# Three scattered edits around the end of an attention loop: stores on another queue, a norm eleven steps later, a diagonal built in two halves

## The chip, the core and the metric

The program runs on one core of one Trainium2 chip. The metric is device time in microseconds (us). A core has five engines that each work through their own instructions in program order: TensorE (PE, matmuls; PEld is its weight load), VectorE (DVE), ScalarE (ACT), GpSimd (POOL) and SyncE (SP). SP computes nothing here: it issues DMA transfers, one behind the other, and an issue that has to wait holds up all that stand behind it. ACT and POOL can issue DMAs too, between their own computations. Operands lie in SBUF, matmul results in PSUM, which has eight banks of 128x512 float32.

## The reference

One encoder layer for 2048 tokens of width 1024, in float32: a mixer with 8 stick-breaking heads and 8 chunked softmax heads, and a squared-ReLU MLP, each behind an RMS norm with shift, scale and gate from a conditioning vector.

```python
h = rmsnorm(x, g_norm1) * (1.0 + sc1) + sh1
proj = h @ w_in                                # q, k, v of both kinds of head
# stick-breaking head: s < t strictly
log_beta, log_1m = log_sigmoid(z), where(strict, log_sigmoid(-z), 0)
w = where(strict, exp(log_beta + (reverse_cumsum(log_1m) - log_1m)), 0);  o_sb = w @ v
# softmax head: own chunk of 64 and the 8 before it, relative bias
o_ca = softmax(q k / 8 + bias) @ v
x = x + gt1 * (concat(o_sb, o_ca) @ w_o)
h = rmsnorm(x, g_norm2) * (1.0 + sc2) + sh2
x = x + gt2 * (square(relu(h @ w1)) @ w2)
```

## The kernel before, in words

Float32 products are made from high and low parts: ACT casts the high part (`wth`, `os`), DVE or POOL subtracts it for the low part (`wtl`), and three matmuls go over the parts. The kernel has three stages: projections (0 to about 425 us), attention (to about 1277 us) and, behind the rest of the output projection, the MLP (to 2524 us).

**Groups and units.** The 2048 tokens are four groups of 512, g = 0 to 3. The attention loop takes the groups 2 and 3 together, then 1, then 0. For a group it runs 8 stick-breaking heads and then 8 softmax heads. A unit of work is one head of one group (for stick-breaking heads, against one block of 512 keys); it has four steps. A step issues score matmuls (`z`, or `ct` and `cz` for softmax), the soft part, and, eight steps later, four or eight transposes (`wt`) and products with the values (`acc`). In a stick-breaking step the soft part is a sigmoid on ACT, a scan on DVE (`p`) and a difference on POOL (`b`). In a softmax step it is a score with bias on DVE (`s`, with `cols` for row values), an exponential on ACT (`e`) and a multiply on POOL (`e<-e,cols`). The last group, g = 0, has one unit for each head, and its softmax heads are the end of the loop.

**Filler.** Each step also issues some matmuls of other work, so that PE has something to do while soft parts are under way. In the last group this is the output projection of group 1: eight tiles `po`, 24 matmuls each, with a weight tile `ow` each; a finished tile is added to the residual by DVE (`xr<-po`, line 229) and stored. What is left of it when the steps are through is issued behind them, and then the projection of group 0 (`pso`) from tiles `opm` that are read back from memory, then the MLP (`ps`).

**A head's result.** `finish` (line 746) puts two heads together in a tile `o` on POOL; `keep` (line 770) splits it into `os` (ACT casts, POOL subtracts) and stores it to `scr_m`, 512 KB, from SP's queue (line 775); only the very last unit uses ACT's queue. `opm` reads these stores.

**The second norm.** For groups 2 and 3 the squares of the projected rows are summed while the projection runs (`finish_row`, line 1160). When the eighth row is in, a chain of jobs follows: `second` makes four column sums on PE (`pvm`); `powers` forms mean and inverse root on four columns (`nvm` on DVE, five tiny POOL operations on `nym` and `ntm`); `spread` multiplies the identity by them on DVE (`ndgm`, 128x512, both inputs in SBUF); `third` spreads the result over the partitions with four matmuls (`prm`); and DVE copies it to SBUF (`r`). `later.add(n, job)` runs a job n steps from now. Groups 0 and 1 have their norm in the MLP, by other code.

**Banks.** Four PSUM banks (tag `z`) serve `z`, `ct`, `cz` and `wt`. Two (tag `ps`) serve `po`, `pvm` and `prm`; a tile that wants one waits until the tile before in it has been read. Two more hold `acc`.

**Order.** ACT, DVE, POOL and PE keep the order in which the code issues (their instructions all show the helper's line 42). SP's order is set by a scheduler that places each DMA.

Of the kernel before, what the change touches and what calls it, by code (L numbers as in the profile page):

```python
# [9 lines left out]
F32 = mybir.dt.float32  # L10
# [3 lines left out]
ALU = mybir.AluOpType  # L14
# [4 lines left out]
P = 128  # L19
# [6 lines left out]
TB = 512  # L26
# [53 lines left out]
def encoder_kernel(ctx, tc, xs, c, g1, g2, w_in, w_first, w_rest, gqk, bias, w_o, w1, w2, w_ada, b_ada, out):  # L80
    nc = tc.nc
    act, dve, pool, sp = nc.scalar, nc.vector, nc.gpsimd, nc.sync
# [34 lines left out]
    ident = cpool.tile([P, P], F32, name="ident")  # L117
# [21 lines left out]
    later = Later()  # L139

    def split(hi, lo, src, lo_eng=None):
        act.copy(hi, src)
        (lo_eng or dve).tensor_tensor(lo, src, hi.bitcast(F32), op=ALU.subtract)
# [22 lines left out]
    def norm_columns(pp, acc, tg):  # L166
        pv = pp.tile([P, TB], F32, tag="ps", name=f"pv{tg}")
        for i in range(4):
            pe.matmul(pv[:, i : i + 1], acc[:, i * P : (i + 1) * P], ones[:, 0:1], start=True, stop=True)
        return pv  # L170

    def norm_powers(pl, pv, tg):
        v = pl.tile([P, 4], F32, tag="nv", name=f"nv{tg}")
        dve.tensor_scalar(v, pv[:, 0:4], 1.0 / D, EPS, op0=ALU.mult, op1=ALU.add)
        y = pl.tile([P, 4], F32, tag="ny", name=f"ny{tg}")
        t = pl.tile([P, 4], F32, tag="nt", name=f"nt{tg}")
        rsqrt(y, v, t)
        return y

    def norm_diagonal(pl, y, tg, home=None):  # L180
        if home is None:
            dg = pl.tile([P, 4, P], F32, tag="ndg", name=f"ndg{tg}", bufs=1)
        else:
            dg = home.rearrange("p (a b) -> p a b", b=P)
        dve.tensor_tensor(
            dg, ident.unsqueeze(1).to_broadcast([P, 4, P]), y.unsqueeze(2).to_broadcast([P, 4, P]), op=ALU.mult
        )
        return dg
# [40 lines left out]
    def residual(g, n, ps, xr):  # L229
        dve.scalar_tensor_tensor(xr, ps, mod[:, 2 * KT + n : 2 * KT + n + 1], xr, op0=ALU.mult, op1=ALU.add)  # L230
        stores.append(lambda: sp.dma_start(scr_x[g, n], xr))
# [12 lines left out]
    if True:  # L244
# [252 lines left out]
        act, dve, pool = (Ordered(tc, e) for e in (act, dve, pool))  # L497
# [70 lines left out]
        dg = np_.tile([P, 4, P], F32, tag="ndg", name="ndga3", bufs=1)  # L568
# [61 lines left out]
        sp = osp  # L630
# [78 lines left out]
    if True:  # L709
# [7 lines left out]
        sp = nc.sync  # L717
# [28 lines left out]
        def finish(u):  # L746
            r = (u.h % 2) * HD
            q = HD - r
            if u.h % 2 == 0:
                pend["o", u.g] = op.tile([P, TB], F32, tag="o", name=f"o{u.nm}")  # L750
            o = pend["o", u.g]
            tmp = op.tile([P, TB], F32, tag="otmp", name=f"otmp{u.nm}")
            rows = slice(r, r + HD)
            act.copy(tmp[rows, :], u.acc[q : q + HD, :])

            def rest():
                act.copy(o[rows, :], u.acc[rows, :])
                soon.append(add)

            def add():  # L760
                pool.tensor_tensor(o[rows, :], o[rows, :], tmp[rows, :], op=ALU.add)
                if u.h % 2:
                    wait({3: 6, 0: 2}.get(u.g, 4), lambda: keep(u, o))

            soon.append(rest)
# [4 lines left out]
        def keep(u, o):  # L770

            os = fp.tile([P, 2, TB], F32R, tag="st", name=f"os{u.nm}")
            split(os[:, 0, :], os[:, 1, :], o, pool)
            q = act if u is units[-1] else sp
            q.dma_start(scr_m[u.g, u.ca * 4 + u.h // 2], os.bitcast(F32))
            if u.ca and u.h == NH - 1 and u.g > 0:
                filler.append(Filler(outproj, u.g))
# [382 lines left out]
        def finish_row(g, n, ps, xr):  # L1160

            residual(g, n, ps, xr)
            if g < 2 and drain:
                return
            stores.pop()()
            if g < 2:
                return

            def square():
                sq = rows[g] if n == 0 else op.tile([P, TB], F32, tag="otmp", name=f"sq{g}_{n}")  # L1170
                act.activation(sq, xr, AF.Square)
                if n:
                    soon.append(lambda: add(sq))

            def add(sq):
                pool.tensor_tensor(rows[g], rows[g], sq, op=ALU.add)
                if n == KT - 1:
                    later.add(3, second)

            def second():  # L1180
                pv = norm_columns(dense, rows[g], f"m{g}")

                def powers():
                    y = norm_powers(op, pv, f"m{g}")
                    later.add(2, lambda: spread(y))

                later.add(1, powers)

            def spread(y):
                dg = norm_diagonal(op, y, f"m{g}", op.tile([P, TB], F32, tag="otmp", name=f"ndgm{g}"))  # L1190
                later.add(2, lambda: third(dg))

            def third(dg):
                pr = dense.tile([P, TB], F32, tag="ps", name=f"prm{g}")
                for i in range(4):
                    pe.matmul(pr[:, i * P : (i + 1) * P], ones, dg[:, i, :], start=True, stop=True)
                later.add(1, lambda: dve.tensor_copy(rows[g], pr))

            if n == 0:
                rows[g] = rp.tile([P, TB], F32, tag="r", name=f"r{g}")  # L1200
            soon.append(square)
# [5 lines left out]
        units = []  # L1207
# [103 lines left out]
        op = ph.enter_context(tc.tile_pool(name="op", bufs=2))  # L1311
# [14 lines left out]
        for i in range(len(steps) + LAG):  # L1326
# [33 lines left out]
            if i + 1 < len(steps):  # L1360
                u, st = steps[i + 1]
# [8 lines left out]
    sp = osp  # L1370
# [21 lines left out]
    if True:  # L1392
# [375 lines left out]
        def plain(mb, i):  # L1768

            f = len(steps)  # L1770
            steps.extend(Second(mb, i, j) for j in range(NP))
            if i == 6:
                for n, step in enumerate((4, 5, 6, 12)):
                    update(mb, n, f + step, temp, False)
            return f
# [139 lines left out]
        def outer(i, plan):  # L1915

            f = len(steps)
            steps.extend(Outer(i, q, k) for q in range(7) for k in range(HP))
            for g in range(HP // 2):
                for pr, (begin, gap) in plan["load"].items():  # L1920
                    at(begin + gap * g, lambda pr=pr, g=g: half(i, pr, g))
                for pr, (begin, gap) in plan["sum"].items():
                    at(begin + gap * g, lambda pr=pr, g=g: half_sum(i, pr, g))
            for q in range(7):
                at(f + HP * q - 12, steps[f + HP * q].load)
            for pr, b in ((5, "22"), (6, "12"), (2, "11"), (4, "21")):
                s = steps[f + HP * OUTER.index(pr)]
                at(f + HP * OUTER.index(pr) + (1 if b == "22" else -5), lambda s=s, b=b: s.load_x(b))
            return f
# [47 lines left out]
        for mb in (1, 0):  # L1977
# [3 lines left out]
            for j in range(NP):  # L1981
                f = steps[begin + 7 * j]
# [41 lines left out]
        f = plain(0, 1)  # L2024
# [4 lines left out]
        for i in DOUBLE:  # L2029
            f = outer(i, plan)  # L2030
# [120 lines left out]
```

## Time and profile before

| what | value |
|---|---|
| runs | 2527.75, 2527.54, 2524.98 us (median 2527.54) |
| profiled execution | 2525.42 us, of which the span is 2523.7 us |
| granted TensorE clock | 1.000 |
| PE busy | 2503.5 us (99%) |
| DVE busy | 2034.2 us (81%) |
| ACT busy | 1523.1 us (60%) |
| POOL busy | 773.8 us (31%) |

A row of a timeline has a start, a length, the engine, the operation, what it writes from what it reads, and how many were joined; in brackets stands the time that the engine was idle just before, and what it waited for. Lengths of joined rows overlap a little with their neighbours, since matmuls are pipelined. Rows of SPq are DMA issues; the length is that of issuing, not of the transfer.

### The profile page before, as it was taken

To read this page: it belongs to the slowest core of one execution; us is meant where nothing else is said; L and a number is where in the kernel's file an instruction comes from. 1 tells how busy PE (TensorE), PEld (TensorE's weight loads), DVE (VectorE), ACT (ScalarE), POOL (GpSimd) and SP (SyncE) were. 2 spreads that over 40 slices of the span, in tenths; PEclk is the share of its full clock that TensorE was granted. 3 is DMA by queue.
4 is the path that set the end of the run, shared out by engine and by line. 5 is a ranking of instruction groups with operands and counts; after the bars stand their busy time and mean duration, and the time that the engine had idled before them with its cause. 6 is when DMAs were issued, how large, how long until landed. Compare 5 with 4: busy or idle time off the path is not lost.

```text
span 2523.7 us, 39531 instructions
## 1 busy us (share of the span) xinstructions
PE 2503.5 (99%) x12384; PEld 2093.8 (83%) x12384; DVE 2034.2 (81%) x3580; ACT 1523.1 (60%) x2917; POOL 773.8 (31%) x1156
## 2 busy tenths in 40 slices
PE   9999999999999999999999999999999999999999
PEld 7888888888888888888888888888888888888787
DVE  7656776887789888999858777779877859799998
ACT  6333424778876687666855555567555546576665
POOL 4330154776776677776620000000000000010000
PEclk9999999999999999999999999999999999999999
DMA  9879968789888788866787878996998996887882
GB/s 369 322 297 362 356 270 292 233 256 315 260 260 252 246 250 252 278 194 206 219 304 254 301 285 316 331 352 189 326 328 270 315 365 260 315 252 278 310 275 83
DMA packets 296547, 706.29 MB, mean 280 GB/s; under 512 B 32016, under 2 KB 88336, under 8 KB 284688
## 3 DMA queue, kind: packets, MB, share of 16 engines
q1 hardware_dynamic: 290432, 690.64, 79.5%
q0 software_dynamic: 4608, 8.39, 1.9%
q10 hardware_dynamic: 1296, 4.72, 0.5%
q8 instruction: 98, 1.61, 0.3%
q14 instruction: 113, 0.93, 0.1%
HBM read 476.61 MB, written 227.02 MB: 279 GB/s over the span
## 4 chain that ended last, share of the span: by engine, by line
PE 87%; DVE 7%; DMA 2%; ACT 1%; issue 1%; SPq 0%; POOL 0%; DVEq 0%; ACTq 0%; POOLq 0%
PE ps L42 25%; PE ps_s L42 15%; PE pt L42 11%; PE acc L42 7%; PE wt L42 7%; PE pf L42 5%; PE z L42 5%; PE po L42 4%; PE pq L42 3%; DVE opr L42 2%; PE pso L42 2%; PE cz L42 2%; DVE ol L42 1%; PE ct L42 1%; DVE r L42 1%
## 5 line engine op out<-in xcount | busy, mean ns | idle before, releaser
L42 ACT CAST wth<-wt 128x512 fp32r<-128x512 f32 (+3 forms) x544 | 257.7, 484 | 177.6 <-PE wt L42 164.7
L42 PE MATMUL ps<-h,opw 128*128 128x512 f32 x1512 | 358.6, 389 | 0.0
L42 DVE TENSOR_TENSOR wtl<-wt,wth 128x512 fp32r<-128x512 f32 (+3 forms) x544 | 291.7, 548 | 66.9 <-ACT wth L42 63.2
L42 POOL TENSOR_TENSOR b<-p 128x512 f32<-128x512 f32 (+1 forms) x320 | 292.0, 912 | 155.8 <-DVE p L42 103.5
L42 PEld LDWEIGHTS ps<-h,opw 128*128 128x128 f32 x1512 | 283.7, 188 | 58.8
L42 PE MATMUL pt<-w,ht 128*128 128x512 f32 x1248 | 288.2, 391 | 0.0
L42 PE MATMUL ps_s<-h,opw 128*128 128x512 f32 x1152 | 277.1, 389 | 0.0
L42 PEld LDWEIGHTS pt<-w,ht 128*128 128x128 f32 x1248 | 233.0, 188 | 47.7
L42 DVE TENSOR_TENSOR_SCAN p<-z,p,zero 128x512 f32<-128x512 f32 x192 | 245.5, 1280 | 20.1 <-ACT z L42 17.4
L42 PEld LDWEIGHTS ps_s<-h,opw 128*128 128x128 f32 x1152 | 216.0, 188 | 45.0 <-DVE cp L42 0.2
L42 ACT CAST opr<-r 128x512 fp32r<-128x512 f32 x280 | 174.3, 623 | 129.1 <-PE ps L42 71.4
L42 PE MATMUL ps<-opr,ol 128*128 128x512 f32 x960 | 222.0, 390 | 0.4 <-DVE opr L42 0.3
L42 PE MATMUL acc<-wth,v 128*128 128x512 f32 (+3 forms) x544 | 221.3, 410 | 0.2
L42 PEld LDWEIGHTS ps<-opr,ol 128*128 128x128 f32 x960 | 179.8, 188 | 40.2 <-DVE opr L42 1.9
L42 ACT ACTIVATE z<-z 128x512 f32<-128x512 f32 (+1 forms) x320 | 166.6, 521 | 54.1 <-PE z L42 49.5
L42 DVE TENSOR_TENSOR opr<-r,opr 128x512 fp32r<-128x512 f32 x280 | 188.5, 704 | 10.7 <-ACT opr L42 9.9
L42 PE MATMUL acc<-wtl,v 128*128 128x512 f32 (+3 forms) x544 | 185.5, 347 | 0.1
L42 PE MATMUL z<-k,q 128*128 128x512 f32 (+3 forms) x640 | 183.1, 368 | 1.5 <-DVE p L42 1.5
L42 POOL DMA_DIRECT2D scr_x<-txu x12 | 10.5, 879 | 546.6 <-ACT txu L42 529.2
L42 PE MATMUL ps<-oph,opv 128*128 128x512 f32 x768 | 175.5, 390 | 0.5 <-DVE txo L42 0.2
L42 PE MATMUL wt<-ident,b 128*128 128x128 f32 x1088 | 170.8, 272 | 1.5 <-DVE p L42 1.5
L42 PEld LDWEIGHTS wt<-ident,b 128*128 128x128 f32 x1088 | 137.2, 140 | 39.9 <-DVE p L42 2.2
(226 smaller groups left out, 5063.9 us busy)
## 6 DMA issues: line engine op xcount, KB each, us to landing
r<-scr_hid SPq DMA_DIRECT2D x80, 512.0 KB, 6.6
q<-scr_q SPq DMA_DIRECT2D x128, 256.0 KB, 5.2
w<-in_w_dram SPq DMA_DIRECT2D x64, 512.0 KB, 5.8
k<-scr_k SPq DMA_DIRECT2D x240, 128.0 KB, 4.3
v<-scr_v SPq DMA_DIRECT2D x120, 256.0 KB, 4.3
wa<-in_w_ada_dram SPq DMA_DIRECT2D x48, 512.0 KB, 6.3
ow<-scr_wo SPq DMA_DIRECT2D x24, 1024.0 KB, 6.5
l<-scr_t SPq DMA_DIRECT2D x20, 1024.0 KB, 7.4
```

Of the source, the lines that this page charges most:

```text
L42: return lambda *x, **y: self.tc.keep_in_program_order(f(*x, **y))
```

## The change

Three edits, in `keep` and in `finish_row`.

1. The stores of `os` for the softmax heads 1, 3 and 5 of the last group (`scr_m` 4, 5 and 6 of group 0) go to POOL's queue instead of SP's.
2. The jobs of group 3's norm start 14 steps behind its last row instead of 3.
3. In the norms of groups 2 and 3 the `ndgm` tile is written by two DVE operations of 128x256, one step apart, and `prm` comes one step later.

```diff
             split(os[:, 0, :], os[:, 1, :], o, pool)
-            q = act if u is units[-1] else sp
+            q = act if u is units[-1] else pool if u.ca and u.g == 0 else sp
             q.dma_start(scr_m[u.g, u.ca * 4 + u.h // 2], os.bitcast(F32))
...
                 if n == KT - 1:
-                    later.add(3, second)
+                    later.add(14 if g == 3 else 3, second)
...
             def spread(y):
-                dg = norm_diagonal(op, y, f"m{g}", op.tile([P, TB], F32, tag="otmp", name=f"ndgm{g}"))
-                later.add(2, lambda: third(dg))
+                dg = op.tile([P, TB], F32, tag="otmp", name=f"ndgm{g}").rearrange("p (a b) -> p a b", b=P)
+
+                def part(i):
+                    dve.tensor_tensor(
+                        dg[:, i : i + 2], ident.unsqueeze(1).to_broadcast([P, 2, P]),
+                        y[:, i : i + 2].unsqueeze(2).to_broadcast([P, 2, P]), op=ALU.mult,
+                    )
+
+                part(0)
+                later.add(1, lambda: part(2))
+                later.add(3, lambda: third(dg))
```

How the order moves is shown at three places. In a name the digits are the kind of head (0 stick-breaking, 1 softmax), the head, the group and the step; `nvm3` and `ndgm3` are group 3's norm, and a last number of five digits only tells tiles apart.

DVE, at the turn from the last stick-breaking head (7) of group 0 to its first softmax head, before:

```order
L42 TENSOR_TENSOR wtl0_7_0_1_3_15291<-wt0_7_0_1_3_15279,wth0_7_0_1_3_15290 128x512
L42 TENSOR_SCALAR nvm3_15303<-pvm3_15264 128x4
L42 SCALAR_TENSOR_TENSOR p0_7_0_3_1_15318<-z0_7_0_3_1_15297,p0_7_0_2_1_15199,zero_254 128x512
L42 TENSOR_TENSOR wtl0_7_0_1_2_15324<-wt0_7_0_1_2_15312,wth0_7_0_1_2_15323 128x512
L42 SCALAR_TENSOR_TENSOR p0_7_0_3_2_15343<-z0_7_0_3_2_15330,p0_7_0_2_2_15223,zero_254 128x512
L42 TENSOR_TENSOR wtl0_7_0_1_1_15349<-wt0_7_0_1_1_15337,wth0_7_0_1_1_15348 128x512
L42 TENSOR_TENSOR ndgm3_15360<-ident_247,nym3_15305 128x512
L42 SCALAR_TENSOR_TENSOR p0_7_0_3_3_15368<-z0_7_0_3_3_15354,p0_7_0_2_3_15243,zero_254 128x512
```

The same place now:

```order
L42 TENSOR_TENSOR wtl0_7_0_1_3_15287<-wt0_7_0_1_3_15275,wth0_7_0_1_3_15286 128x512
L42 SCALAR_TENSOR_TENSOR p0_7_0_3_1_15305<-z0_7_0_3_1_15293,p0_7_0_2_1_15200,zero_254 128x512
L42 TENSOR_TENSOR wtl0_7_0_1_2_15311<-wt0_7_0_1_2_15299,wth0_7_0_1_2_15310 128x512
L42 SCALAR_TENSOR_TENSOR p0_7_0_3_2_15330<-z0_7_0_3_2_15317,p0_7_0_2_2_15224,zero_254 128x512
L42 TENSOR_TENSOR wtl0_7_0_1_1_15336<-wt0_7_0_1_1_15324,wth0_7_0_1_1_15335 128x512
L42 SCALAR_TENSOR_TENSOR p0_7_0_3_3_15353<-z0_7_0_3_3_15341,p0_7_0_2_3_15244,zero_254 128x512
```

`nvm3` and `ndgm3` are gone from between the scans. The two halves now stand on DVE between the scores of the third softmax head (2), where before only the scores and the low parts stood:

```order
L42 TENSOR_TENSOR ndgm3_15709<-ident_247,nym3_15619 128x256
L42 ISA s1_2_0_2_15684,cols_264<-cz1_2_0_2_15703,bias2_0_15381,cols_264 128x384
L42 ISA cols_264 128x1
L42 ISA s1_2_0_3_15721,cols_264<-ct1_2_0_1_15667,bias2_0_15381 128x256
L42 ISA cols_264 128x1
L42 RECIPROCAL cols_264<-cols_264 128x1
L42 TENSOR_TENSOR wtl1_0_0_0_15726<-wt1_0_0_0_15714,wth1_0_0_0_15725 128x128
L42 TENSOR_TENSOR wtl1_0_0_5_15730<-wt1_0_0_5_15716,wth1_0_0_5_15729 128x384
L42 TENSOR_TENSOR ndgm3_15709<-ident_247,nym3_15619 128x256
```

On PE, `pvm3` and `prm3` move in the same way. Before, `prm3` stood in the turn, ahead of the start of the next filler tile `po1_1`:

```order
L42 MATMUL cz1_0_0_1_15421<-k1_0_0_15154,q1_0_0_15151 128x384 x2
L42 MATMUL prm3_15424<-ndgm3_15360,ones_252 128x128 x4
L42 MATMUL wt0_7_0_2_2_15429<-ident_247,b0_7_0_2_0_15166 128x128
L42 MATMUL wt0_7_0_2_2_15429<-ident_247,b0_7_0_2_1_15198 128x128
L42 MATMUL wt0_7_0_2_2_15429<-ident_247,b0_7_0_2_2_15222 128x128
L42 MATMUL wt0_7_0_2_2_15429<-ident_247,b0_7_0_2_3_15242 128x128
L42 MATMUL acc0_7_0_0_15255<-wth0_7_0_1_1_15348,v0_7_0_1_15104 128x512
L42 MATMUL acc0_7_0_0_15255<-wtl0_7_0_1_1_15349,v0_7_0_1_15104 128x512
L42 MATMUL cz1_0_0_2_15449<-k1_0_0_15154,q1_0_0_15151 128x384 x2
L42 MATMUL po1_1_15456<-fx7_0_14863,ow1_1_14986 128x512 x3
```

It now stands some 125 rows further on, at softmax head 3, inside the filler tile `po1_2`:

```order
L42 MATMUL ct1_3_0_1_15829<-k1_3_0_15500,q1_3_0_15497 128x256 x4
L42 MATMUL cz1_3_0_1_15834<-k1_3_0_15500,q1_3_0_15497 128x384 x2
L42 MATMUL po1_2_15782<-fx7_1_14866,ow1_2_15184 128x512
L42 MATMUL prm3_15838<-ndgm3_15709,ones_252 128x128 x4
L42 MATMUL wt1_1_0_2_15843<-ident_247,e1_1_0_0_15523 128x128
```

With that, `po1_1` has its bank free at the turn, where it had to wait for the residual `xr1_0` to be read out of the other one.

On SP's queue, at the end of the loop, before:

```order
L740 DMA v1_6_0_16336<-scr_v1_1_1_155 128x512
L775 DMA scr_m0_5_165<-os1_3_0_16502 128x1024
L740 DMA v1_7_0_16478<-scr_v1_0_1_153 128x512
L740 DMA v1_7_0_16478<-scr_v1_1_1_155 128x512
L775 DMA scr_m0_6_166<-os1_5_0_16688 128x1024
L42 DMA opm0_0_16969<-scr_m0_0_160 128x1024
L42 DMA opm0_1_16971<-scr_m0_1_161 128x1024
L42 DMA opm0_2_16973<-scr_m0_2_162 128x1024
L42 DMA opm0_3_16975<-scr_m0_3_163 128x1024
L42 DMA ow1_6_16978<-scr_wo6_236 128x2048
```

and now:

```order
L740 DMA v1_6_0_16338<-scr_v1_1_1_155 128x512
L740 DMA v1_7_0_16480<-scr_v1_0_1_153 128x512
L740 DMA v1_7_0_16480<-scr_v1_1_1_155 128x512
L42 DMA opm0_0_16971<-scr_m0_0_160 128x1024
L42 DMA opm0_1_16973<-scr_m0_1_161 128x1024
L42 DMA opm0_2_16975<-scr_m0_2_162 128x1024
L42 DMA opm0_3_16977<-scr_m0_3_163 128x1024
L42 DMA ow1_6_16980<-scr_wo6_236 128x2048
```

The four reads `opm` and the weights `ow1_6` no longer stand behind the two stores. On POOL's queue the stores stand right behind the subtraction that completes their tile:

```order
L42 TENSOR_TENSOR o1_4_0_16508<-o1_4_0_16508,otmp1_5_0_16607 64x512
L42 TENSOR_TENSOR os1_5_0_16690<-o1_4_0_16508,os1_5_0_16690 128x512
L42 DMA scr_m0_6_166<-os1_5_0_16690 128x1024
L42 TENSOR_TENSOR o1_6_0_16694<-o1_6_0_16694,otmp1_6_0_16695 64x512
L42 TENSOR_TENSOR o1_6_0_16694<-o1_6_0_16694,otmp1_7_0_16727 64x512
L42 TENSOR_TENSOR os1_7_0_16731<-o1_6_0_16694,os1_7_0_16731 128x512
```

In this queue the store of heads 4 and 5 now comes ahead of the sum and the split of heads 6 and 7.

## The prediction

> **What bounds the kernel now.** I read the page's sums first, then PE's waits over the whole run, then windows around the places that the change touches.
>
> ```profile
> PE 2503.5 (99%) x12384; PEld 2093.8 (83%) x12384; DVE 2034.2 (81%) x3580; ACT 1523.1 (60%) x2917; POOL 773.8 (31%) x1156
> ```
>
> PE is busy 2503.5 of 2523.7 us, so about 20.2 us is all that any reordering can win. The waits say where the larger pieces lie:
>
> ```profile
> PE po L42 <- DMA ow<-scr_wo: 2.3, 1, 2.3
> PE wt L42 <- DVE p L42: 2.2, 4, 1.1
> PE po L42 <- DVE xr L42: 1.4, 1, 1.4
> PE prm L42 <- DVE xr L42: 0.5, 1, 0.5
> ```
>
> The first, third and fourth happen once each; of the second the longest piece is 1.1. The windows (length, then busy time of PE, PEld, DVE, ACT, POOL with counts, clock, DMA share, GB/s) put them in time:
>
> ```profile
> 1180.00:1200.00 20.00, 17.42 (x106) 14.71 (x105) 16.28 (x34) 10.96 (x20) 12.90 (x19) 1.00 0.44 134
> 1200.00:1220.00 20.00, 20.00 (x129) 17.92 (x127) 16.42 (x59) 14.70 (x33) 11.29 (x9) 1.00 0.72 206
> 1280.00:1300.00 20.00, 17.73 (x79) 14.38 (x78) 5.21 (x8) 4.46 (x8) 1.29 (x1) 1.00 1.00 367
> 1300.00:1350.00 50.00, 50.00 (x222) 41.42 (x221) 45.81 (x75) 28.62 (x47) 0.00 (x0) 1.00 0.87 320
> ```
>
> PE loses 2.58 us at the turn to the softmax heads and 2.27 us at the end of the loop. Behind 1300 it is full, so what is won before that carries to the end.
>
> **The late norm (group 3), at the turn.** DVE and PE there, and POOL:
>
> ```profile
> 1187.64 1.44 DVE L42 TENSOR_TENSOR ndgm<-ident,nym 128x512 f32<-128x512 f32 x1
> 1189.00 1.27 DVE L42 TENSOR_TENSOR_SCAN p<-z,p,zero 128x512 f32<-128x512 f32 x1
> 1196.03 0.68 DVE L42 COPY r<-prm 128x512 f32<-128x512 f32 x1
> 1190.33 0.66 PE L42 MATMUL wt<-ident,b 128*128 128x128 f32 x4 [1.08 <-DVE p L42]
> 1192.47 1.05 PE L42 MATMUL prm<-ndgm,ones 128*128 128x128 f32 x8
> 1196.17 1.89 PE L42 MATMUL po<-fx,ow 128*128 128x512 f32 x7 [1.40 <-DVE xr L42]
> 1187.24 1.28 POOL L42 TENSOR_TENSOR o<-o,otmp 64x512 f32<-64x512 f32 x1
> ```
>
> The scan starts when `ndgm` ends; `b` and the transposes follow it. Without `ndgm` the scan can start 1.36 earlier (1189.00 less 1187.64), more than the wait of 1.08 behind it: that wait goes. The wait of 1.40 is `po1_1` waiting for the residual, because `prm` holds the other of the two banks; now that bank is free, and the wait goes too. Sum 2.48, nearly all of the window's 2.58. `pvm` and `prm` themselves are not saved: the same matmuls run later, in a stretch where PE is full.
>
> What comes back: DVE has the work in the softmax heads, and POOL the five small powers. POOL is busy 11.29 of 20 there; its multiplies have a lead of eight steps over the transposes, so I cost POOL nothing. DVE gets `ndgm` in two halves of 0.35 or somewhat more (next part), the copy's 0.68 and the four columns of `nvm`: some 1.5 us. It is free 3.58 of 20 us there, and the seven steps from `pvm` to the copy take some 16 us (a step is 2.3: the splits of two heads stand at 1227.27 and 1245.45, eight steps apart), so there is room for about 2.9. How a lump on DVE reaches PE in this stage shows a step that has a residual in it:
>
> ```profile
> 1246.95 0.74 DVE L42 SCALAR_TENSOR_TENSOR xr<-po,mod,xr 128x512 f32<-128x512 f32 x1
> 1248.86 0.74 PE L42 MATMUL ct<-k,q 128*128 128x256 f32 x4 [0.22 <-DVE cols L42]
> ```
>
> 0.74 on DVE cost PE 0.22, so 1.5 costs an estimated 0.45. Bounds: 0 (all in gaps) and 4.0 (below, the lock). Net of this edit: -2.0.
>
> **The halves.** How long one takes is open; the group of the whole ones shows:
>
> ```profile
> L42 DVE TENSOR_TENSOR ndgm<-ident,nym x4: 692/1058/1435, 1042.9 to 1565.9; 128x512 f32<-128x512 f32 x4
> ```
>
> Twice it takes 0.69, twice about 1.43, and those two are in the attention loop, where POOL is at work (here `o`, from 1187.24 to 1188.52; `ndgm` outlasts that by 0.56). So a half is 0.35 alone and 0.35 plus the rest of a POOL operation otherwise. Two halves can meet two POOL operations where a whole one meets one. The Trainium skill, "SBUF — State Buffer", section "SBUF: two separate sides", has this as an exclusive lock: a DVE operation with two SBUF inputs and a GpSimd operation that reads SBUF do not share, the later one waits for the whole of the earlier. By that rule the split speaks against the change, and the trace agrees as far as 1.43 against 0.69 goes; the second rival is what it would cost. In group 2 the norm stays where it was; there
>
> ```profile
> 1046.52 1.16 PE L42 MATMUL prm<-ndgm,ones 128*128 128x128 f32 x8 [0.52 <-DVE xr L42]
> 1048.83 0.69 DVE L42 TENSOR_TENSOR wtl<-wt,wth 128x512 fp32r<-128x512 f32 x1 [0.85 <-ACT wth L42]
> ```
>
> `prm` waited 0.52 for a residual that stands behind `ndgm`. With half of that ahead of the residual, and `prm` a step later, the wait goes; the second half then delays the next scan and its scores. Bounds -0.52 (goes, nothing follows) and +0.5 (as much again behind the second half); I take -0.3, nearer the lower one, since DVE was idle for 0.85 just behind.
>
> **The stores.** SP's queue, its waits, what PE did, the chain, and POOL:
>
> ```profile
> SPq L775 <- POOL os L42: 12.8, 2, 8.2
> 1267.61 0.80 SPq L740 DMA_DIRECT2D v<-scr_v  x2
> 1276.60 0.32 SPq L775 DMA_DIRECT2D scr_m<-os  x1
> 1277.02 2.17 SPq L42 DMA_DIRECT2D opm<-scr_m  x4
> 1279.29 0.39 SPq L42 DMA_DIRECT2D ow<-scr_wo  x1
> 1275.34 0.45 PE L42 MATMUL po<-fx,ow 128*128 128x512 f32 x1
> 1277.12 11.12 PE L42 MATMUL po<-fx,ow 128*128 128x512 f32 x48
> 1290.51 11.16 PE L42 MATMUL po<-fx,ow 128*128 128x512 f32 x48 [2.27 <-DMA ow<-scr_wo]
> 1279.29 11.09 DMA ow<-scr_wo
> 1301.67 43.52 PE pso L42 x192
> 1275.29 1.28 POOL L42 TENSOR_TENSOR os<-o,os 128x512 fp32r<-128x512 f32 x1 [2.58 <-ACT os L42]
> ```
>
> SP stood 8.2 us before the store of heads 4 and 5, and behind it four reads of 512 KB and the weights `ow` that PE then lacked for 2.27 us. Now the reads go out right behind `v`, at about 1268.4 (times of the run before; everything is some 2.5 earlier). At 367 GB/s their 2.1 MB take 5.7 us, so they are through by 1276. `ow` takes over a tile whose last reader is the filler matmul at 1275.34, so it is issued at about 1275.9 instead of 1279.29, and with nothing ahead of it. Its kind lands in
>
> ```profile
> DMA to landing us min/median/max: 4.7/6.5/11.1
> ```
>
> so at 1280.6 to 1287.0, and PE wants it at 1288.24 (1277.12 + 11.12). The 2.27 go, with 1.2 to spare even at the longest. What is late next is `opm` 4 to 7; their issue moves up with the queue, by some 3 us or more.
>
> POOL now issues three DMAs. The nearest rows are its stores in the MLP, of half the size:
>
> ```profile
> L42 POOL DMA_DIRECT2D scr_x<-cs x16: 844/1009/1200, 1766.0 to 2273.0; - x16
> DMA to landing us min/median/max: 4.0/7.4/10.8
> 1227.27 1.28 POOL L42 TENSOR_TENSOR os<-o,os 128x512 fp32r<-128x512 f32 x1 [0.40 <-ACT os L42]
> 1245.45 1.29 POOL L42 TENSOR_TENSOR os<-o,os 128x512 fp32r<-128x512 f32 x1 [0.73 <-ACT os L42]
> ```
>
> An issue costs POOL 0.84 to 1.2, up to 2.4 if it grows with size. Behind the first two stand multiplies with eight steps of lead; behind the third stand the sum and the split of heads 6 and 7, whose tile (`opm` 7) is wanted in `pso`, from 1301.67 on, some 25 us later. I cost all three at nothing; the cover would have to fall by more than ten us before they showed. Net of this edit: -2.27.
>
> **Sum.** -2.48 + 0.45 - 0.3 - 2.27 = -4.6 us. The profiled execution took 2525.42; less 4.6 that is 2520.8. The median of the runs is 2527.54, 2.1 above the profiled one, so on its scale I predict 2522.9. The bound of 0.2%, about what a measurement of this kernel tells from no change, is 5.05 us: the forecast lies just inside it.
>
> **Rivals.**
> - More is won. All of group 2's 0.52 goes, and nothing comes back from DVE: -2.48 - 0.52 - 2.27 = -5.3, or 2522.2. For it: DVE's 3.58 free us. Against: the row with 0.22.
> - The halves meet POOL's multiplies, of which there are four a head:
>
> ```profile
> L42 POOL TENSOR_TENSOR e<-e,cols x30: 1243/1254/1257, 1200.7 to 1266.4; 128x640 f32<-128x640 f32 x30
> ```
>
>   Each half waits up to a multiply's 1.25, so DVE gets 1.5 + 2.5 = 4.0 us, more than the 2.9 free. At the rate of 0.22 in 0.74 it costs 1.2, and at the worst all 4.0: -3.85 to -1.05, or 2523.7 to 2526.5. For it: 1.43 against 0.69, and POOL at 11.29 of 20. Against: a half that starts while POOL is idle waits for nothing. This is the case that the Trainium skill's lock (the section named above) would give whenever a half starts inside a multiply.
> - The last head's values come late. PE's first use of them, and the landing of the two DMAs that were issued from 1267.61 on:
>
> ```profile
> 1272.60 0.45 PE L42 MATMUL acc<-wth,v 128*128 128x512 f32 x1
> DMA to landing us min/median/max: 2.7/2.8/3.0
> ```
>
>   They were there at about 1271.2, with some 1.4 us to spare. Now 2.1 MB of reads follow at once. If the transfers share instead of queueing, all 2.6 MB go at 367 GB/s and `v` lands up to 7 us after its first issue, 1274.7: PE loses up to 2.1, and the sum is -2.5, or 2525.0. Against: `ow`, issued behind the four reads, took its 11.09 us, as if it came last of them.
> - Slower: POOL's store of heads 4 and 5 lands late. It leaves at about 1277.6, and `opm` 6 reads it; PE wants that tile 18 matmuls into the first `pso` (of 24 at 0.227, from 43.52 over 192), at 1305.8 less the 2.27 won, 1303.5. A read of 512 KB takes about 7 us, so the store may land until 1296, 18.8 us after its issue, before it costs anything; from 23.4 us on it costs all of the 4.6, and at 30 us the kernel takes 2534. The longest landing in POOL's row is 10.8. In the same section the Trainium skill warns that DMAs from this queue can starve while DVE holds the port, its descriptors being written by GpSimd; no row of this kernel shows it.
>
> **How the numbers follow.** Forecast 0.55, half of it beyond the bound of 0.2% as the forecast lies 0.4 us from it; more won 0.13; halves meet POOL 0.15; late values 0.09; slower 0.08, in which I count the unseen as well. That gives faster by over 0.2%: 0.27 + 0.13 = 0.40; within: 0.28 + 0.15 + 0.09 = 0.52; slower: 0.08. The range runs from the larger win with group 2 and 3 us for run-to-run scatter (the three runs lie 2.8 apart) to the worst of the lock with a little over: 2519.0 to 2527.0; what it leaves out is the slower rival and a tail on both sides.
>
> **What would show it.** In the profile after: no wait of PE for `xr` and none over 0.3 for `p` near 1187; `ow` issued before the loop's last matmuls end, with no wait behind it; PE at 19.8 or more of 20 in both windows; `ndgm` x2 for each norm at 0.35 to 0.9. Waits of `ct` for `cols` between 1210 and 1225 of more than 0.5 in sum would show the lock; a wait of `acc` for `v` near 1270 or of `pso` for `opm` the two DMA rivals. The prediction is wrong if the waits return elsewhere before 1345, or if the MLP loses what the loop won, its loads being timed to PE.

## The result, and the profile after

The changed kernel takes 2520.5 us (median of 10 runs, 2519.28 to 2522.5), the kernel before 2526.25 us (10 runs, 2524.53 to 2527.87). The ratio is 0.9979, with a 95% interval of 0.9971 to 0.9988: faster by 0.21%, 5.3 us by the ratio and 5.75 by the medians. The prediction said 2522.9, 2519.0 to 2527.0. The profiled execution after took 2520.14 us, its span is 2518.4.

From PE's waits in the whole run, the three with the largest sums in the attention stage, and the windows that answer to those of before:

```profile
PE z L42 <- DVE p L42: 2.0, 6, 0.6
PE wt L42 <- DVE p L42: 1.2, 3, 0.4
PE cz L42 <- DVE cols L42: 0.3, 1, 0.3
```

```profile
1180.00:1200.00 20.00, 19.94 (x120) 17.23 (x119) 17.98 (x43) 14.31 (x27) 13.05 (x18) 1.00 0.57 173
1200.00:1220.00 20.00, 19.66 (x129) 17.77 (x128) 17.44 (x62) 13.96 (x31) 12.62 (x15) 1.00 0.74 217
1280.00:1300.00 20.00, 20.00 (x90) 16.57 (x89) 10.95 (x17) 6.35 (x10) 0.00 (x0) 1.00 0.96 347
```

The waits of `po` for `ow` (2.3), of `po` for `xr` (1.4), of `prm` for `xr` (0.5) and the long one of `wt` for `p` (1.1) are gone. PE loses 0.06 us and nothing where it lost 2.58 and 2.27, and loses 0.34 between 1200 and 1220, where group 3's norm now stands.

The parts of the change are 2 to 3 us each, no more than the scatter between runs. To see them all the same, I measure three stretches between starts of PE rows that every version has. *Group 2* runs from the column sums of group 2's norm (1036.16 before) to the `z` matmuls ahead of the turn (1179.74); the *turn* from there to the row of filler behind the loop's last values (1277.12); the *end* from there to the first `pso` (1301.51). Where versions have the same work in a stretch, repeats agree within about 0.1, and within 0.2 at the end where PE waits for `ow` (24.18 to 24.39). Each version's time stands beside that of the kernel before on the same chip; "(one)" marks a single execution.

| kernel | group 2 | turn | end | time, kernel before | ratio (95%) |
|---|---|---|---|---|---|
| before | 143.58 | 97.38 | 24.39 | | |
| the whole change | 143.63 | 94.71 | 21.84 | 2520.50, 2526.25 | 0.9979 (0.9971 to 0.9988) |
| e1 stores only | 143.58 | 97.37 | 21.84 | 2523.57, 2525.46 | 0.9992 (0.9983 to 1.0001) |
| e2 late norm only | 143.63 | 94.72 | 24.26 | 2522.94, 2525.46 | 0.9988 (0.9979 to 0.9997) |
| e3 halves only | 143.63 | 97.29 | 24.20 | 2526.28, 2525.46 | 1.0003 (0.9994 to 1.0012) |
| e4 stores and late norm | 143.55 | 94.71 | 21.84 | 2519.67, 2525.46 | 0.9977 (0.9968 to 0.9986) |
| e5 stores on ACT's queue | 143.59 | 99.95 | 23.43 | 2527.65, 2526.15 | 1.0005 (0.9996 to 1.0014) |
| e6 last store only | 143.50 | 94.71 | 21.84 | 2520.30, 2526.15 | 0.9979 (0.9970 to 0.9988) |
| e7 POOL beside `ndgm` | 143.61 | 94.73 | 21.84 | 2519.33 (one), 2526.15 | |
| e8 diagonals by ACT | 142.79 | 94.79 | 21.84 | 2520.11, 2526.15 | 0.9976 (0.9967 to 0.9986) |
| e9 norm 3 left out | 143.57 | 92.69 | 21.82 | 2519.12, 2525.79 | 0.9973 (0.9962 to 0.9984) |
| e10 `prm` late | 143.60 | 95.77 | 25.76 | 2524.85 (one), 2525.79 | |
| e11 diagonal late | 143.57 | 94.38 | 24.18 | 2522.32 (one), 2525.79 | |
| e12 best parts | 142.76 | 94.58 | 21.83 | 2519.92, 2525.32 | 0.9976 (0.9966 to 0.9986) |

For the change that is +0.05, -2.67 and -2.55, in sum -5.17 us. Behind `pso` nothing changes: from the first `pso` to the last row of `ps_s` it is 1206.08 before (1301.51 to 2507.59) and 1206.14 after (1296.74 to 2502.88).

**The end.** SP's queue, then PE and POOL's stores, after:

```profile
1257.61 8.57 SPq L740 DMA_DIRECT2D v<-scr_v  x4
1266.28 1.80 SPq L42 DMA_DIRECT2D opm<-scr_m  x4
1273.59 0.32 SPq L42 DMA_DIRECT2D ow<-scr_wo  x1
1274.90 22.00 PE L42 MATMUL po<-fx,ow 128*128 128x512 f32 x96
L42 POOL DMA_DIRECT2D scr_m<-os x3: 602/612/800, 1244.8 to 1274.6; - x3
DMA to landing us min/median/max: 3.0/8.2/8.4
```

The reads of `opm` are out 8.6 us ahead of PE's last filler row, where they stood level with it before (1277.02 against 1277.12); `ow` is issued 1.3 us ahead of that row instead of 2.2 behind it. The two groups of 48 matmuls have become one of 96.

**The turn and the halves.** DVE's scan, PE, then group 3's halves with the POOL multiplies beside them and what PE saw of it:

```profile
1187.24 1.27 DVE L42 TENSOR_TENSOR_SCAN p<-z,p,zero 128x512 f32<-128x512 f32 x1
1188.68 0.60 PE L42 MATMUL wt<-ident,b 128*128 128x128 f32 x4
1191.98 1.78 PE L42 MATMUL po<-fx,ow 128*128 128x512 f32 x7
1211.20 0.79 DVE L42 TENSOR_TENSOR ndgm<-ident,nym 128x256 f32<-128x256 f32 x1
1213.68 0.94 DVE L42 TENSOR_TENSOR ndgm<-ident,nym 128x256 f32<-128x256 f32 x1
1210.45 1.25 POOL L42 TENSOR_TENSOR e<-e,cols 128x640 f32<-128x640 f32 x1 [0.47 <-DVE cols L42]
1213.09 1.25 POOL L42 TENSOR_TENSOR e<-e,cols 128x640 f32<-128x640 f32 x1 [1.38 <-DVE cols L42]
1215.21 0.62 PE L42 MATMUL cz<-k,q 128*128 128x384 f32 x2 [0.34 <-DVE cols L42]
```

The transposes and the first matmuls of `po1_1` run without a wait. Each half ends 0.28 to 0.29 behind the end of the multiply beside it (1211.99 against 1211.70, 1214.62 against 1214.34): it waited for POOL each time and then took about 0.3.

**Group 2.** DVE and PE after:

```profile
1043.33 1.17 DVE L42 TENSOR_TENSOR ndgm<-ident,nym 128x256 f32<-128x256 f32 x1
1046.54 0.64 DVE L42 TENSOR_TENSOR ndgm<-ident,nym 128x256 f32<-128x256 f32 x1
1047.83 0.73 PE L42 MATMUL z<-k,q 128*128 128x512 f32 x2 [0.56 <-DVE p L42]
1048.64 1.05 PE L42 MATMUL prm<-ndgm,ones 128*128 128x128 f32 x8
```

`prm` no longer waits 0.52, but a step earlier `z` waits 0.56 for the scan behind the second half. The halves take 1.81 together, where the whole one took 1.42.

### The profile page after: what moved, and what is told of

It is laid out like the page before. It is cut to its first block, busy times and chain, and to the rows that moved or that the text cites. A ratio compares the mean times of both kernels' runs of the same rounds, so it can differ in the third digit from the quotient of the medians.

```text
span 2518.4 us, 39536 instructions
## 1 busy us (share of the span) xinstructions
PE 2502.6 (99%) x12384; PEld 2093.5 (83%) x12384; DVE 2034.9 (81%) x3582; ACT 1523.2 (60%) x2917; POOL 777.1 (31%) x1159
## 3 DMA queue, kind: packets, MB, share of 16 engines
q8 instruction: 98, 1.61, 0.3%
## 4 chain that ended last, share of the span: by engine, by line
PE 86%; DVE 8%; DMA 2%; ACT 2%; issue 2%; SPq 0%; POOL 0%; DVEq 0%; ACTq 0%; POOLq 0%
PE ps L42 24%; PE ps_s L42 14%; PE pt L42 11%; PE acc L42 7%; PE wt L42 7%; PE pf L42 5%; PE po L42 5%; PE z L42 5%; PE pq L42 3%; DVE opr L42 2%; PE pso L42 2%; PE cz L42 2%; DVE ol L42 1%; DVE r L42 1%; PE ct L42 1%
## 5 line engine op out<-in xcount | busy, mean ns | idle before, releaser
L42 PEld LDWEIGHTS ps<-oph,opv 128*128 128x128 f32 x768 | 144.0, 188 | 31.0 <-DVE txo L42 0.6
```

Source lines behind the costliest of these rows:

```text
L42: return lambda *x, **y: self.tc.keep_in_program_order(f(*x, **y))
```

## The experiments

**Each part alone, and the two that count together.** The theory: the late norm gives the turn, the stores give the end, the halves give nothing. The rival: the parts need each other (the halves so that the late norm does not stall the softmax heads, the earlier turn so that the reads land).

```diff
# e1, on the kernel before
-            q = act if u is units[-1] else sp
+            q = act if u is units[-1] else pool if u.ca and u.g == 0 else sp
# e2, on the kernel before
-                    later.add(3, second)
+                    later.add(14 if g == 3 else 3, second)
# e3, on the kernel before: the third edit of the change, whose last lines are
...
+                part(0)
+                later.add(1, lambda: part(2))
+                later.add(3, lambda: third(dg))
# e4: e1 and e2
```

> Only the three stores go to POOL's queue; the norms stand as before. I measure two stretches on PE: the turn, from the z matmuls just ahead of the place where pvm3 stood to the first of the last filler matmuls (97.4 us before, 94.7 with the whole change), and the end, from there to the first pso (24.4 before, 21.8 with the whole change). If the stores are worth the wait for ow and nothing else: turn 97.4, end 21.8, and the kernel 2.6 us faster than before. If the reads of opm need the earlier turn too to land in time: end 23 to 24.4 and the kernel less than 1.5 us faster.

> Only group 3's norm comes eleven steps later, its diagonal in one piece; stores on SP's queue. If the turn's gain is the late norm alone: turn 94.7, end 24.4, kernel 2.6 us faster than before. If the halves are needed to keep the norm from stalling PE in the softmax heads (one piece of 1.4 us or more between scores): turn 95.2 to 96 and waits of ct or cz for cols of 0.5 to 1.3 more.

> Only the diagonals of groups 2 and 3 in two halves, at the old places; stores on SP's queue. If the halves gain nothing: turn 97.4 within 0.4, end 24.4, group 2's wait of prm for xr replaced by one of z for p of about the same 0.5, kernel within 0.5 us of before. If each half waits for a POOL operation: the two halves of group 3 take 1.6 to 2.4 in sum at the turn, and the turn is 97.6 to 98.4. If the halves help: turn 96.4 or less, since the scan behind the first half starts earlier.

> Stores on POOL's queue and the late norm, diagonals in one piece. If the two parts add and the halves give nothing: turn 94.7, end 21.8, kernel 5.2 us faster than before, as with the whole change. If the halves matter in the softmax heads: turn 95.2 to 96, kernel 4.0 to 4.7 faster.

The stretches add to the tenth: e1 has the whole change's end (21.84) and the old turn (97.37), e2 its turn (94.72) and the old end (24.26), e4 both, and e3 neither. So the halves are worth nothing, and the rival falls. e2 has the norm's diagonal in one piece among the softmax scores; PE's waits from 1160 to 1310 there are

```profile
PE po L42 <- DMA ow<-scr_wo: 2.1, 1, 2.1
PE prm L42 <- DVE xr L42: 0.2, 1, 0.2
PE ct L42 <- DVE cols L42: 0.2, 1, 0.2
```

0.22 at `prm` instead of the 0.34 at `cz` with halves. e3's halves at the old place give no wait less either: `wt` for `p` 0.8, `cz` for `cols` 1.0, `prm` for `xr` 0.7, and a turn of 97.29.

e1's time is only 1.9 us below that of the kernel before, with 2.55 less in its end; its interval reaches 1.0001, so by time alone the stores are not shown to gain. Its profile has a wait of 0.9 of `ps_s` for ACT in the MLP that the kernel before and the whole change do not have, and e12's has one of 1.0; what brings it on was not found.

**What at the turn costs.** My reading had two waits of separate cause, the diagonal ahead of the scan and the bank that `prm` holds.

```diff
# e10, on the kernel before: prm and the copy four steps later
-                later.add(2, lambda: third(dg))
+                later.add(6 if g == 3 else 2, lambda: third(dg))
# e11, on the kernel before: diagonal, prm and copy eight steps later
-                    later.add(2, lambda: spread(y))
+                    later.add(10 if g == 3 else 2, lambda: spread(y))
# e9, on the whole change: group 3's norm left out
-                if n == KT - 1:
-                    later.add(14 if g == 3 else 3, second)
+                if n == KT - 1 and g == 2:
+                    later.add(3, second)
```

> The kernel before, with one edit: of group 3's norm prm and the copy alone come four steps later, behind the start of po1_1; pvm, the powers and the whole diagonal stay at the turn. By my theory the turn has two separate waits. The one of po1_1 for xr (1.40) is the bank that prm holds, so it goes; the one of wt for p (1.08) is the diagonal ahead of the scan, so it stays: turn 95.9 to 96.2 (97.4 before, 94.7 with the late norm). If the bank is not the cause and DVE is simply late throughout: the wait of 1.40 stays, turn 97.2 or more. If one of the two carries the other: turn 94.7 or 97.4.

> The kernel before, with one edit: group 3's diagonal, prm and copy come eight steps later, pvm and the powers stay where they were, three steps behind the last row. If diagonal and bank are all that costs at the turn: both waits gone, turn 94.7 as with the late norm, and the eleven steps for pvm and the powers give nothing. If pvm and the powers cost something there too (POOL's 1.9 us, nvm on DVE): turn 95.0 to 95.6.

> The whole change, but group 3's norm is left out behind its sum of squares (no pvm, powers, diagonal, prm and copy), so its rows are not normalised. It prices what the change moved. If it costs only its matmuls (1.7) and the one wait of 0.3: turn 92.7, and the kernel 2.0 us faster than the whole change. If it costs more in hidden ways (DVE's 2.6 us spread over steps): turn 91.0 to 92.3.

e10, PE, the one wait left at the turn:

```profile
1190.41 0.66 PE L42 MATMUL wt<-ident,b 128*128 128x128 f32 x4 [1.09 <-DVE p L42]
```

With `prm` alone moved the wait of 1.40 is gone and that of 1.09 stays; the turn is 95.77, 1.61 shorter. With the diagonal moved too (e11) both are gone and the turn is 94.38, 3.00 shorter, 0.33 better than with the whole norm late. Each of the two ran once, so they are read by their waits and stretches and not by their times. So it is the bank and the diagonal, each for its part, and `pvm` and the powers did no harm where they were: moving them gains nothing.

e9 prices the norm at both places. Without it the turn is 92.69. With it late it is 94.71, which is 2.02 more: about 1.7 for the matmuls (0.79 for `pvm` and 0.89 for `prm` in the chain of the whole change) and 0.34 of waiting. At the old place it was 97.38, 4.69 more: the same 1.7, and 3.0 of stall.

**Which store, and which queue.**

```diff
# e6, on the whole change: only the store of heads 4 and 5
-            q = act if u is units[-1] else pool if u.ca and u.g == 0 else sp
+            q = act if u is units[-1] else pool if u.ca and u.g == 0 and u.h == 5 else sp
# e5, on the whole change: ACT's queue
-            q = act if u is units[-1] else pool if u.ca and u.g == 0 else sp
+            q = act if u.ca and u.g == 0 else sp
```

> The whole change, but only the store of heads 4 and 5 goes to POOL's queue; those of heads 0 to 3 stay on SP's. In the profile of before SP stood 8.2 us at that one and 4.6 at the one ahead of it, which stands ahead of v of head 7. If the gain is the blocked reads behind the last store: end 21.8, time as the whole change within 0.3. If the one ahead of it counts too (v of the last head late): a wait of acc for v near 1270 or an end of 22.5 to 24.

> The whole change, but the three stores go to ACT's queue instead of POOL's. A store waits for POOL's subtraction, which ends 1.3 us or more behind ACT's cast, and on ACT's queue the casts and exponentials of the softmax heads stand behind it. If leaving SP's queue is all that counts: turn 94.7, end 21.8, same time as the whole change. If the wait holds up ACT: ACT idle for 1 to 2 us at each of the three stores, waits of PE for wth or e behind them, turn 95.5 to 98 and the kernel 1 to 3 us slower than the whole change.

e6 has the same end, 21.84, and the same time as the whole change. SP's row for the store of heads 2 and 3 stands where it stood, and the reads follow `v` at once:

```profile
1263.00 0.32 SPq L775 DMA_DIRECT2D scr_m<-os  x1
1265.32 0.80 SPq L740 DMA_DIRECT2D v<-scr_v  x2
1266.16 1.85 SPq L42 DMA_DIRECT2D opm<-scr_m  x4
```

`v` waits for PE to release its tile and not for that store. One store of the three does it all.

On ACT's queue (e5) the end's cause is gone as well, and still the kernel loses 6.8 us in the two stretches against the whole change, far more than I expected. ACT at the first of the three stores, PE behind it and behind the third, and windows there:

```profile
1244.69 0.58 ACT L42 COPY otmp<-acc 64x512 f32<-64x512 f32 x1 [1.76 <-POOL os L42]
...
1246.27 1.07 PE L42 MATMUL wt<-ident,e 128*128 128x128 f32 x8 [1.70 <-DVE wtl L42]
...
1279.03 0.38 PE L42 MATMUL acc<-wth,v 128*128 128x256 f32 x1 [1.88 <-ACT wth L42]
...
1279.89 23.60 PE L42 MATMUL po<-fx,ow 128*128 128x512 f32 x96
```

```profile
1276.00:1280.00 4.00, 2.05 (x14) 1.49 (x13) 1.30 (x4) 1.83 (x5) 1.59 (x2) 0.99 0.75 247
1280.00:1284.00 4.00, 4.00 (x12) 3.15 (x12) 0.29 (x1) 1.78 (x3) 2.83 (x3) 0.58 0.87 301
```

ACT stands 1.76 us at each store (5.3 in sum), with the casts that PE waits for behind it; and after the last stall the granted clock falls to 0.58 of full over four us, so that the 96 matmuls take 23.60 instead of 22.00. Which queue the stores go to is thus worth more here than leaving SP's (6.8 us against 2.55): on POOL each store stands right behind the subtraction that it waits for, with 0.30 to 0.33 us of idle time ahead of the issue.

**The wait between DVE and POOL.** The attention loop showed `ndgm` at 1.43 beside POOL and 0.69 in the MLP, which might have had other causes.

```diff
# e7, on the whole change, in the MLP's norm2 (group 1: tb = 1, group 0: tb = 0)
+                busy = (lambda: pool.tensor_tensor(acc, acc, acc, op=ALU.add)) if tb else (lambda: pool.memset(acc, 0.0))
-                dg = norm_rstd(padl, fresh, acc, f"m{tb}", None, np2.tile(...))
+                dg = norm_rstd(padl, fresh, acc, f"m{tb}", busy, np2.tile(...))
```

> The whole change, and in the MLP, where POOL has nothing to do and the two whole ndgm of groups 1 and 0 take 0.69 us, an extra POOL operation starts just ahead of each: for group 1 an add of 128x512 that reads and writes SBUF (on a tile that is free there), for group 0 a memset of the same size, which reads nothing. If the port is locked against POOL operations that read SBUF: group 1's ndgm takes 1.4 to 1.9 (0.69 plus nearly all of the add's 1.0 to 1.3), group 0's 0.69. If the two engines share: group 1's about 0.9 to 1.2 and the add longer than 1.3. If both slow down alike, the memset holds the port too. If both stay at 0.69, the 1.4 in the attention loop had another cause.

```profile
1476.48 1.04 POOL L42 TENSOR_TENSOR r<-r 128x512 f32<-128x512 f32 x1
1476.56 1.50 DVE L42 TENSOR_TENSOR ndgm<-ident,nym 128x512 f32<-128x512 f32 x1 [2.27 <-POOL nym L42]
1561.57 0.53 POOL L42 MEMSET r<- 128x512 f32 x1
1561.67 0.69 DVE L42 TENSOR_TENSOR ndgm<-ident,nym 128x512 f32<-128x512 f32 x1 [2.31 <-POOL nym L42]
```

Beside the add, which takes its own 1.04, `ndgm` takes 1.50 and ends 0.54 behind it; beside the memset it takes 0.69. It waits for a POOL operation that reads SBUF, whole, and does not share. This is the exclusive lock of the Trainium skill, "SBUF — State Buffer", "SBUF: two separate sides", with its exception for operations that do not read; these runs agree with both.

**Better versions.**

```diff
# e8, on the whole change: the diagonals of groups 2 and 3 by ACT, in place of DVE's operation
...
+                    for j in range(i, i + 2):
+                        act.activation(dg[:, j, :], ident, AF.Copy, scale=y[:, j : j + 1])
# e12: e8 with group 3's pvm and powers at the old place, diagonal, prm and copy eight steps later
...
+                    later.add(10 if g == 3 else 2, lambda: spread(y))
```

> The whole change, with the diagonals of groups 2 and 3 made by ACT (a copy of the identity scaled by one column, four of 128x128, two a step) instead of DVE. DVE gets about 1.8 us less at each norm, ACT some 1.2 more. If what is left of the norms' waits is DVE's lumps: the wait of z for p near 1047 (0.56) and those of cz and ct for cols (0.3 and 0.2) go, and the kernel is 0.5 to 1.0 us faster than the whole change. If ACT's lump does the same to its casts: no gain, or up to 0.5 slower.

> A version put together from the runs before: stores on POOL's queue, diagonals of groups 2 and 3 made by ACT in two steps, group 3's pvm and powers at their old place and only diagonal, prm and copy late (by eight steps). If the parts add: group 2's stretch (from pvm2 to the z ahead of the turn, 143.6 before and with the change) 142.8, turn 94.4, end 21.8, and the kernel 1.1 us faster than the whole change, 6.3 faster than before. If ACT's four copies stall the softmax heads: turn 94.7 or more, no faster than with ACT's diagonals alone.

```profile
L42 ACT ACTIVATE ndgm<-ident,nym x8: 387/390/403, 1042.5 to 1213.6; 128x128 f32<-128x128 f32 x8
```

ACT makes a column block in 0.39, with no long one among the eight (387 to 403 ns). Group 2's stretch falls to 142.79 and PE waits nowhere in it, so its wait was the diagonal's; the turn does not fall (94.79). e12's turn, 94.58, does not reach e11's 94.38; that ACT's copies give back some of what they spare DVE would fit, but was not shown. Neither is faster in time than the whole change by more than the intervals: 0.9976 against 0.9979. The 0.8 us of group 2 are seen in the stretch and not shown in the time.

## Why the prediction held, term by term

**The sum.** It said -4.6; the stretches say -5.17, the times -5.3 to -5.75. The direction and both main mechanisms were right, and the time lies in the range. The 0.21% lie just beyond the 0.2% at which the forecast was in doubt, and its interval (0.12 to 0.29%) holds both sides. Of the 2.4 us between 2522.9 and 2520.5, 1.3 is the base: the forecast started from the median of three runs (2527.54), and that of ten is 2526.25. The size comes nearest to the rival "more is won" (-5.3), but not by its terms: group 2 gave nothing and 0.34 came back, and instead each long stall was worth more than it was read.

**The late norm at the turn: right, its size too small.** The prediction took the two waits, 2.48, as what goes, and 0.45 as what comes back. e10 and e11 show the two waits with the causes that it gave. What went is 3.0 (4.69 less the 1.7 of matmuls, e9), and 0.34 comes back. The step that was short is reading a stall by the idle time in its bracket. Rows of matmuls that follow without a gap overlap, and a wait ends that: at the end of the loop the two rows of 48 took 11.12 and 11.16, in sum 22.28, and the one of 96 takes 22.00. The row behind a wait is somewhat longer too: `po` x7 took 1.89 behind its wait and 1.78 without, `prm` 1.16 (group 2, waiting) and 1.05. At the end the sum of both can be read cleanly: the bracket says 2.27 and the stretch gains 2.55, in e2 2.15 and 2.42, in e3 2.08 and 2.36. A wait there costs 0.27 to 0.28 more than its bracket.

**What comes back: nearly right.** The estimate of 0.45, from a residual that put 0.74 on DVE and cost PE 0.22, stands against 0.34. POOL's five small powers cost nothing that e9 shows beyond that.

**The halves: the rival was half right.** Both halves of both norms did wait for a POOL operation; the lock is real (e7), and the pair is longer than the whole one (1.73 and 1.81 us against 1.44 and 1.42). The rival's price, 1.2 or more on PE, did not come: the two halves of group 3 cost PE 0.34, and the late norm in one piece (e2, e4) gives the same turn.

**Group 2: wrong by 0.3.** I took -0.3 of a range of -0.52 to +0.5; it was +0.05. The step that failed is the choice within the range: DVE's idle 0.85 lies behind two more scans, and the scan that `z` waits for stands right behind the second half.

**The stores: right, again short by the 0.28.** `ow` was to be issued at 1275.9 on the old clock; it is at 1273.59, 2.3 ahead of that, as everything there is 2.2 ahead. POOL's issues were priced at 0.84 to 2.4 and took 0.60 to 0.80, with nothing of it on PE. That all three stores must go was not the prediction's claim, and one is enough (e6).

**The rivals on the transfers did not come.** `v` landed without a wait of PE for it, with 2.1 MB of reads at its heels; the longest landing of a POOL store was 8.4, against the 18.8 from which it would have cost anything.

**Open.** The medians differ by 0.6 us more than the stretches. The two profiles cannot explain that: their spans differ by 5.3, since the one after reaches group 2's column sums 0.4 later (1036.56 against 1036.16) and ends 0.6 sooner behind DVE's last operation (3.7 against 4.3), both scatter that no run ties to the change. A part may be the clock. Of the 81 runs of the kernel before beside e1 to e12, 35 have a mean granted clock of 1.000 (one halved window of 3.4 us takes 0.0007 off it) and take 2524.21 to 2526.41 us, and 17 have 0.998 and take 2526.51 to 2529.27; of the 69 runs of the versions without the wait for `ow` and without e5's stalls none has 0.998. So the long waits of the kernel before seem to halve its clock for a while in some of its runs, as in e10 below; how much of the 0.6 that is was not worked out.

## What to carry to other kernels

When an in-order DMA queue stands still, look at what stands behind the blocked issue: one store that waits for a slow producer held up four reads and the weights that the bound engine wanted, and issuing that store from its producer's own queue cost nothing here, while issuing it from another busy engine's queue moved the blockage there. A small side job on the path is best cut at its resource: here a PSUM bank and one vector operation in front of a scan made the whole price, the rest of the job could stay. Measure such parts between marks on the bound engine's timeline, where repeats agree to 0.1 us, when run times scatter by three.

## What the runs showed that I had not expected

A short stall of PE can cost more than itself by halving the granted clock behind it. In e10 PE waits 2.07 us for `ow` as the kernel before does, and the 48 matmuls behind it take 12.75 us instead of 11.16:

```profile
1288.77 12.75 PE L42 MATMUL po<-fx,ow 128*128 128x512 f32 x48 [2.07 <-DMA ow<-scr_wo]
```

```profile
1286.00:1288.00 2.00, 0.69 (x4) 0.23 (x2) 0.00 (x0) 0.00 (x0) 0.00 (x0) 1.00 1.02 417
1288.00:1290.00 2.00, 1.24 (x4) 1.07 (x5) 0.65 (x1) 0.00 (x0) 0.00 (x0) 0.84 1.03 431
1290.00:1292.00 2.00, 2.00 (x6) 1.53 (x5) 0.10 (x1) 0.00 (x0) 0.00 (x0) 0.50 0.88 324
1292.00:1294.00 2.00, 2.00 (x8) 1.60 (x8) 0.01 (x1) 0.00 (x0) 0.00 (x0) 0.80 0.97 326
```

The clock column falls to 0.50 and is back some 3 us later; the price is 1.6 us. The same happened in e5 behind a stall of 1.88, and it accounts for e10's end of 25.76 against 24.39. It did not happen behind 2.27 in the profile of before, 2.15 in e2 or 2.08 in e3, so the length of the stall alone does not decide it. The Trainium skill, "TensorE: Matmul & The Clock Gate", Part 1, has a clock that is halved by a monitor with a window of about 3.4 us that runs freely; a stall would then count by how it lies in that window.

The traces bear this out. In each of them the times at which the granted clock changes lie whole multiples of 3.413 us apart, which gives the windows of that run. The windows that hold all or most of the stall are, in e10, e5, before and e3:

```profile
1285.96:1289.37 3.41, 1.34 (x7) 0.82 (x6) 0.02 (x1) 0.00 (x0) 0.00 (x0) 1.00 1.03 426
1276.50:1279.91 3.41, 1.46 (x9) 0.90 (x7) 0.90 (x3) 1.59 (x4) 1.32 (x2) 1.00 0.74 235
1286.35:1289.76 3.41, 1.90 (x9) 1.24 (x7) 0.00 (x0) 0.00 (x0) 0.00 (x0) 1.00 0.99 399
1289.15:1292.56 3.41, 1.58 (x7) 1.35 (x8) 0.75 (x1) 0.00 (x0) 0.00 (x0) 1.00 1.04 423
```

PE is busy for 0.39 and 0.43 of the first two windows, and the clock is 0.50 for the whole window behind; it is busy for 0.56 and 0.46 of the other two, and the clock stays at 1.00. Behind the first 20 us of each of the 14 traces no window breaks this order: 0.43 or less is followed by 0.50, and 0.44 or more by 1.00. In the first 20 us two windows do (0.46 in e6 and 0.67 in e4, both followed by 0.50). The table of that section of the Trainium skill puts half clock behind an idle window; here a window that was a little under half busy was enough, so a stall of 1.88 us that lay within one window cost more than one of 2.27 that was split between two. No run was made that only shifts a stall against its windows.
